# A hybrid mixer and SwiGLU trunk on one core: GpSimd's elementwise work given to VectorE, and one PSUM tile taken from another pool

## The chip, the core and the metric

The kernel runs on one core of a Trainium2 chip. Five engines work from queues of their own: TensorE (PE) multiplies matrices into PSUM, VectorE (DVE) and ScalarE (ACT) read PSUM and do elementwise work, GpSimd (POOL) does elementwise work on SBUF, and SyncE (SP) issues transfers. They meet at semaphores. The metric is the device time of one execution in microseconds, the median of several runs.

## The reference, cut to what matters

Two layers, 512 frames of 1024 channels, float32. Each layer is a token mixer followed by a SwiGLU feed-forward; both are normed before and after and added to the residual. The mixer is one projection whose columns feed three branches:

```python
q, k, v = silu(conv4(dn_qkv)); q, k l2-normed            # 4 heads of 128
beta = sigmoid(dn_b); g = -exp(A_log) * softplus(dn_a + dt_bias)
o_dn = gated_delta_rule(q, k, v, beta, g)                # chunks of 64, a triangular solve in each
o_dn = rms(o_dn) * dn_out_norm * silu(dn_z)
o_pool = mapped(trailing means over 2, 4, 8, 16 frames, minus the frame) * scale
rq, rk = rotary(ret_q), rotary(ret_k)
o_ret = groupnorm(chunkwise_retention(rq, rk, ret_v)) * ret_out_norm * silu(ret_g)
y = sigmoid(g0)*(o_dn @ w_dn) + sigmoid(g1)*(o_pool @ w_pool) + sigmoid(g2)*(o_ret @ w_ret)
x = x + rms_norm(y @ w_out);  x = x + rms_norm(swiglu(rms_norm(x)))
```

Inside a chunk the delta rule solves `(I + M) X = rhs` with a strictly lower triangular `M = (k_beta k^T) * decay`. Retention weights frame j for frame i by gamma^|i-j| within a chunk and by gamma^(i-j) across chunks.

## The kernel before, in words

All activations lie channel by frame: 128 partitions, 512 columns, eight tiles for 1024 channels. A projection (L515 to L522, `project`) makes 128 output channels: eight pieces of 128 input channels, and for each piece three matmuls of 512 columns (`mm3`, L231 to L233), because each float32 operand is held as a rounded high part and a remainder. The weights come as 512 KB tiles over SyncE's queue (L216) and are split in halves of 512 columns: ScalarE rounds (L241, `wh`), VectorE subtracts (L242, `wl`). A PSUM tile `pp` (three buffers) takes a projection, `fx` (two buffers) the small products of retention, pooling and the token gates, `cx` (three buffers) those of the delta rule.

The delta rule (`delta`) is a generator that yields a number of steps; between its parts `fill` advances the lanes `tasks` (projections and what follows them: pooling, rotations, retention, gates, branches), `side` (the attention part of retention) and `late`. So the order in which the program is written comes out of how often each generator yields, and a scheduler then settles the order of every engine's queue, with the weight loads and splits drawn ahead by priorities (`EARLY`, `AHEAD`). Each engine executes its queue in that order, and an instruction that waits holds up what stands behind it.

What the change and the prediction touch:

- `token_gates` (L553): L564 makes the product of the gate columns into `fx`, VectorE scales it (L567, `cv`), TensorE transposes it with selection matmuls (L570) into a second `fx` tile, and ScalarE (L577, `beta`) and VectorE (L579, `sx`) read that tile. The pooling maps L1044 follow in `fx`.
- `sums_of` and the loop behind it (L770, L771, L785 to L787): decays and masks per head, 256 columns each.
- The block inverses of head h are sent through the queue of SyncE into `uc` (L843, four loads per head, 16 in a row). `back` (L934) takes `uc` as `uu` (L944) and runs two level steps per head: transposes L547 and products L960 with a mask `ml` (L938), the product L970, and the subtraction L971 into `uu`.
- `rotated` (L1084) and `retention` (L1098): L1090 to L1094 make `kr` and `qr`. Values are transposed (L547) into a PSUM tile, and their mean is taken off (L1119, L1121, L1123, `vc`). The gate projection gives L1126 and its sigmoid L1128.
- `attention` (L1132): scores L1136 and transposed keys L1138 into two `fx` tiles, read by L1140 (VectorE) and L1141 (ScalarE); the state product L1150 into `fx`; the running states (L1152 on ScalarE, two L1154 on VectorE); L1165 and L1167 for the output.
- `mixed_in` (L1067) adds a branch to `y`.

Of the kernel before, what the change touches and what calls it, by code (L numbers as in the profile page):

```python
# [135 lines left out]
def tile_hybrid(ctx: ExitStack, tc: tile.TileContext, x_in, consts, rot, rmask, vecs, wab, wi, wpl, wbr, wo, wgu, wd, out):  # L136
# [30 lines left out]
    def over(m, n=NT):  # L167

        return m.rearrange("p (o b) -> p o b", o=1).to_broadcast([P, n, m.shape[1]])

    def along(s, width):

        return s.rearrange("p (t o) -> p t o", o=1).to_broadcast([P, s.shape[1], width])
# [29 lines left out]
    def hd(t, n=NT):  # L203
        return t.rearrange("p (t b) -> p t b", t=n)
# [325 lines left out]
    def mixer(l, xd, hs, rb, firsts):  # L530
# [5 lines left out]
        def tl(tag, bufs=1, shape=(P, S), dt=F32):  # L536
            return pool.tile(list(shape), dt, tag=tag, bufs=bufs, name=nm(tag))

        def tiny(tag, n=16):
            return tl(tag, shape=(P, n))  # L540

# [11 lines left out]
        def token_gates():  # L553
            raw = tl("mc", 2, (P, NT * B16))
            nc.scalar.dma_start(out=raw, in_=wab[l])
            G.memset(abw.bitcast(F32), 0.0)
            r8, w8 = raw.rearrange("p (k n) -> p k n", n=8), abw.rearrange("p (k n) -> p k n", n=P)
            V.tensor_copy(out=w8[:, :, 0:8], in_=r8)
            V.tensor_tensor(out=w8[:, :, 8:16], in0=r8, in1=w8[:, :, 0:8].bitcast(F32), op=ALU.subtract)
            yield WAITS["ab"]  # L560
            ps = psum_f()
            for k in range(KT):
                for j in range(2):
                    T.matmul(ps, lhsT=w8[:, k], rhs=hs[k][j], start=k == 0 and j == 0, stop=k == KT - 1 and j == 1)  # L564
            yield
            ab = tl("cv")
            V.tensor_tensor(out=ab[0:16, 0:S], in0=ps[0:16], in1=rb[0:16], op=ALU.mult)  # L567
            pst = psum_o()
            for t in range(NT):
                T.matmul(  # L570
                    pst[:, t * 8 : t * 8 + 8], lhsT=ab[0:16, ts(t)], rhs=kc[0:16, K_SEL : K_SEL + 8], start=True, stop=True
                )
            yield
            abt = pst[:, 0:32].rearrange("p (t n) -> p n t", n=8)

            beta = tiny("beta")
            A.activation(out=beta.rearrange("p (n t) -> p n t", n=4), in_=abt[:, 0:4], func=AF.Sigmoid)  # L577
            sx = tiny("sx")
            V.tensor_tensor(  # L579
                out=sx.rearrange("p (n t) -> p n t", n=4),  # L580
                in0=abt[:, 4:8],
                in1=vec[:, l, V_DTB : V_DTB + 16].rearrange("p (n t) -> p n t", n=4),
                op=ALU.add,
            )

            nab = tiny("nab")
            V.scalar_tensor_tensor(out=nab, in0=sx, scalar=-1.0, in1=sx, op0=ALU.mult, op1=ALU.min)
            e = tiny("e")
            A.activation(out=e, in_=nab, func=AF.Exp)
            ea = tiny("ea")  # L590
            with behind(A.engine):
                A.activation(out=ea, in_=vec[:, l, V_ALOG : V_ALOG + 16], func=AF.Exp)
            den = tiny("den")
            V.tensor_scalar(out=den, in0=e, scalar1=2.0, scalar2=None, op0=ALU.add)
            V.reciprocal(out=den, in_=den)
            yield
            z = tiny("z")
            V.tensor_tensor(out=z, in0=e, in1=den, op=ALU.mult)
            z2 = tiny("z2")
            V.tensor_tensor(out=z2, in0=z, in1=z, op=ALU.mult)  # L600
            po = tl("po", 2, (P, 16))
            V.tensor_scalar(out=po, in0=z2, scalar1=2.0 / 17, scalar2=None, op0=ALU.mult)
            for c in (15, 13, 11, 9, 7, 5, 3):
                po2 = tl("po", 2, (P, 16))
                V.scalar_tensor_tensor(out=po2, in0=po, scalar=2.0 / c, in1=z2, op0=ALU.add, op1=ALU.mult)
                po = po2
            yield
            lp = tiny("lp")
            V.scalar_tensor_tensor(out=lp, in0=po, scalar=2.0, in1=z, op0=ALU.add, op1=ALU.mult)
            sp = tiny("sp")  # L610
            V.scalar_tensor_tensor(out=sp, in0=sx, scalar=0.0, in1=lp, op0=ALU.max, op1=ALU.add)
            g = tiny("g")
            V.scalar_tensor_tensor(out=g, in0=sp, scalar=-1.0, in1=ea, op0=ALU.mult, op1=ALU.mult)
            for _ in range(GATES):
                yield
            pcs = psum_c()
            for n, m in enumerate((c_le, c_gt, c_e0, c_e1)):
                T.matmul(pcs[:, n * 16 : n * 16 + 16], lhsT=m, rhs=g, start=True, stop=True)
            yield
            ex = tiny("ex", 64)  # L620
            A.activation(out=ex, in_=pcs[:, 0:64], func=AF.Exp)
            tok.update(beta=beta, g=g, e_g=ex[:, 0:16], e_tail=ex[:, 16:32], e_last=[ex[:, 32:48], ex[:, 48:64]])
            yield
# [18 lines left out]
        def hc(h):  # L642
            return slice(h * NT, (h + 1) * NT)
# [96 lines left out]
        def delta():  # L740
# [26 lines left out]
            def sums_of(h):  # L767
                rr = tl("c1", 4)
                r3 = rr.rearrange("p (a t b) -> p a t b", a=2, t=NT)
                G.tensor_tensor(out=r3[:, 0], in0=over(gt64), in1=along(g[:, hc(h)], C), op=ALU.mult)  # L770
                G.tensor_tensor(out=r3[:, 1], in0=over(le64), in1=along(g[:, hc(h)], C), op=ALU.mult)  # L771
                return rr

            rr = sums_of(0)
# [1 line left out]
            for h in range(H):  # L776
                ps = psum_c()
                T.matmul(ps[:, 0 : NT * C], lhsT=c_le, rhs=rr[:, 0 : NT * C], start=True, stop=True)
                T.matmul(ps[:, NT * C :], lhsT=c_gt, rhs=rr[:, NT * C :], start=True, stop=True)
                dec = tl("c1", 4)  # L780
                A.activation(out=dec, in_=ps, func=AF.Exp)
                if h + 1 < H:
                    rr = sums_of(h + 1)
                bm = tl("bm", 1, half)
                G.tensor_tensor(out=hd(bm), in0=over(gt64), in1=along(brk2[:, hc(h)], C), op=ALU.mult)  # L785
                G.tensor_tensor(out=ms_[h], in0=dec[:, 0 : NT * C], in1=bm, op=ALU.mult)
                G.tensor_tensor(out=hd(ats[h]), in0=hd(dec[:, NT * C :]), in1=over(le64), op=ALU.mult)  # L787
                yield WAITS["dec"]


# [142 lines left out]
        def back(h, m_, uc, beg, e_tail):  # L933
            def level(v):  # L934
                m = tl("ml", 2)
                for f in range(2):
                    cc = slice(f * C, (f + 1) * C)
                    G.tensor_tensor(out=hd(m)[:, :, cc], in0=hd(m_), in1=over(lvl[v][:, cc]), op=ALU.mult)  # L938
                return hd(m)

            ml = level(LEVELS[0])
# [61 lines left out]
            A.activation(out=sg, in_=t, func=AF.Sigmoid)  # L1003
            res.append(sg)


        tl("gap", shape=(P, 16))

        def operand(name, i, fn):
            a, b = tl("oh", H, dt=F32R), tl("ol", H, dt=F32R)  # L1010
            fn(a, b)
# [43 lines left out]
        def mixed_in(i, name, n, r_):  # L1055
            if n % 2 == 0:
                bw[name] = weights(wbr[l, i, n // 2])
            ps = psum_p()
            yield from products(ps, bw[name], [oh[name, k] for k in range(H)], 4 * (n % 2))
            if name == "p":  # L1060
                y = keep.tile([P, S], F32, tag="y", bufs=KT, name=nm("y"))
                V.tensor_tensor(out=y, in0=ps, in1=r_[0], op=ALU.mult)
                ys[n] = y
            else:
                t = ftc()
                V.tensor_tensor(out=t, in0=ps, in1=r_[0], op=ALU.mult)  # L1066
                G.tensor_tensor(out=ys[n], in0=ys[n], in1=t, op=ALU.add)  # L1067
            yield

        crb, srb = tl("crb"), tl("srb")  # L1070
# [14 lines left out]
        def rotated(b, tag, res):  # L1085
            r_ = []
            yield from project(wi[l, b], hs, r_)
            ps = r_[0]
            t1, t2 = ftc(), ftc()
            V.tensor_tensor(out=t1, in0=ps, in1=crb, op=ALU.mult)  # L1090
            V.tensor_tensor(out=t2[0:C], in0=ps[C:P], in1=srb[C:P], op=ALU.mult)
            V.tensor_tensor(out=t2[C:P], in0=ps[0:C], in1=srb[0:C], op=ALU.mult)
            o = tl(tag)
            G.tensor_tensor(out=o, in0=t1, in1=t2, op=ALU.add)  # L1094
            res.append(o)
            yield


        def retention(h):
# [13 lines left out]
            for _ in range(VT):  # L1113
                next(p)
                yield
            ps = psum_f()
            transposed(v_, ps)
            su = tl("rsu", 2, (P, NT))
            V.tensor_reduce(out=su, in_=hd(ps), axis=AX.X, op=ALU.add)  # L1119
# [12 lines left out]
        def attention(h, mask, kr, qr, vc, t, sg):  # L1132
# [6 lines left out]
            s_sb, kt = ftc(), ftc()[:, 0 : S - P]  # L1139
            V.tensor_tensor(out=hd(s_sb), in0=hd(s_ps), in1=over(mask[:, 0:P]), op=ALU.mult)  # L1140
            A.activation(out=kt, in_=k_ps[:, 0 : S - P], func=AF.Copy, scale=mask[:, 2 * P : 2 * P + 1])  # L1141
            G.tensor_tensor(out=hd(qr), in0=hd(qr), in1=over(mask[:, P : 2 * P]), op=ALU.mult)
            sw = tl("sw")
            V.scalar_tensor_tensor(
                out=sw, in0=t, scalar=vec[:, l, V_RN + h : V_RN + h + 1], in1=sg, op0=ALU.mult, op1=ALU.mult
# [327 lines left out]
```

## Time and the profile before

| | us |
|---|---|
| median of 3 runs | 1832.48 (1831.73 to 1835.91) |
| the profiled execution's own time | 1831.59 |
| its span | 1829.8 |
| TensorE busy in it | 1807.6 (99%) |
| VectorE busy | 1049.8 (57%) |
| ScalarE busy | 719.1 (39%) |
| GpSimd busy | 364.1 (20%) |

The span is the time from the first to the last instruction in the trace; 1.8 us lie around it. Matmuls are pipelined, so their recorded lengths overlap: a 512-column matmul is recorded with about 0.39 us, though the next one starts earlier. An idle stretch before an instruction is given with what ended it, as in "[2.29 <-DVE vc L1123]".

### The profile page before, as it was taken

The numbers are of one execution on the slowest core, as the hardware profiler recorded it, in microseconds if no ns is written. First come the engines' busy times: TensorE is split into PE (matmuls) and PEld (weight loads), VectorE is DVE, ScalarE is ACT, GpSimd is POOL, SyncE is SP. The second block draws the span as 40 slices with busy tenths as digits, with TensorE's granted clock in tenths as the row PEclk, the third lists the DMA queues.
The fourth block names the chain that finished last, engine by engine and source line by source line (L and its number), as shares of the span: only waits on it lengthen the run. The fifth ranks groups of instructions, "written<-read, shape, count | busy, mean of one in ns | idle before, by whom it ended". The sixth has DMA issues, their size and how long they took to land.

```text
span 1829.8 us, 25153 instructions
## 1 busy us (share of the span) xinstructions
PE 1807.6 (99%) x9528; PEld 1538.0 (84%) x9528; DVE 1049.8 (57%) x1924; ACT 719.1 (39%) x1294; POOL 364.1 (20%) x350
## 2 busy tenths in 40 slices
PE   9999999999999999999999999999999999999997
PEld 7788888888898888888987888888888988888887
DVE  7778766674447432444577786676644564324443
ACT  5643333333445332333446433333434443333332
POOL 2040211012133210221210402110121332102212
PEclk9999999999999999999999999999999999999998
DMA  5323212124325333233233222222243252323221
GB/s 187 118 71 95 75 62 79 52 93 138 104 82 182 95 98 98 92 104 93 83 131 97 83 84 74 61 73 62 89 142 121 66 179 93 103 92 101 96 93 47
DMA packets 65849, 177.73 MB, mean 97 GB/s; under 512 B 15424, under 2 KB 19648, under 8 KB 65728
## 3 DMA queue, kind: packets, MB, share of 16 engines
q1 hardware_dynamic: 58800, 173.04, 29.3%
q10 hardware_dynamic: 6928, 3.08, 0.7%
q8 instruction: 75, 1.23, 0.3%
q14 instruction: 46, 0.38, 0.1%
HBM read 167.18 MB, written 8.39 MB: 96 GB/s over the span
## 4 chain that ended last, share of the span: by engine, by line
PE 95%; DVE 3%; issue 1%; ACT 0%; DMA 0%; POOL 0%; ACTq 0%; DVEq 0%
PE pp L231 28%; PE pp L233 28%; PE pp L232 28%; PE cx L232 1%; PE cx L231 1%; PE cx L233 1%; PE cx L876 1%; PE fx L276 1%; PE cx L861 1%; PE cx L960 1%; PE cx L970 1%; PE cx L547 1%; PE cx L801 0%; PE cx L898 0%; DVE xt L354 0%
## 5 line engine op out<-in xcount | busy, mean ns | idle before, releaser
L231 PE MATMUL pp<-hh,wh 128*128 128x512 f32 (+1 forms) x1592 | 628.6, 395 | 0.0
L233 PE MATMUL pp<-hh,wl 128*128 128x512 f32 (+1 forms) x1592 | 616.6, 387 | 0.0
L232 PE MATMUL pp<-hl,wh 128*128 128x512 f32 (+1 forms) x1592 | 615.9, 387 | 0.0
L241 ACT ACTIVATE wh<-raw 128x512 fp32r<-128x512 f32 x570 | 355.9, 630 | 648.6 <-PE pp L232 575.2
L242 DVE TENSOR_TENSOR wl<-raw,wh 128x512 fp32r<-128x512 f32 x570 | 424.8, 750 | 298.7 <-ACT wh L241 287.1
L233 PEld LDWEIGHTS pp<-hh,wl 128*128 128x128 f32 x1592 | 299.0, 188 | 62.4 <-issue 1.0
L231 PEld LDWEIGHTS pp<-hh,wh 128*128 128x128 f32 x1592 | 299.3, 188 | 60.9 <-issue 3.7
L232 PEld LDWEIGHTS pp<-hl,wh 128*128 128x128 f32 x1592 | 299.5, 188 | 57.6 <-issue 1.0
L231 PE MATMUL pp<-ah,wh 128*128 128x512 f32 (+1 forms) x376 | 134.7, 358 | 0.0
L233 PE MATMUL pp<-ah,wl 128*128 128x512 f32 (+1 forms) x376 | 134.4, 357 | 0.0
L232 PE MATMUL pp<-al,wh 128*128 128x512 f32 (+1 forms) x376 | 134.4, 357 | 0.0
L1340 POOL TENSOR_TENSOR gs<-gt,sg 128x512 f32<-128x512 f32 x44 | 57.6, 1310 | 315.2 <-ACT sg L1338 315.2
L1345 POOL TENSOR_TENSOR a<-gs,ut 128x512 f32<-128x512 f32 x44 | 70.8, 1612 | 130.8 <-DVE ut L1343 130.8
L314 POOL TENSOR_TENSOR sqa<-sqa,sq 128x256 f32<-128x256 f32 (+1 forms) x73 | 63.8, 874 | 106.0 <-ACT sq L307 83.6
L231 PEld LDWEIGHTS pp<-ah,wh 128*128 128x128 f32 x376 | 71.0, 189 | 10.4
L232 PEld LDWEIGHTS pp<-al,wh 128*128 128x128 f32 x376 | 71.0, 189 | 10.4
L233 PEld LDWEIGHTS pp<-ah,wl 128*128 128x128 f32 x376 | 71.0, 189 | 10.2
L242 DVE TENSOR_TENSOR al<-a,ah 128x512 fp32r<-128x512 f32 x44 | 33.9, 770 | 74.4 <-ACT ah L241 74.2
L231 PE MATMUL pp<-yh,wh 128*128 128x256 f32 (+1 forms) x224 | 67.1, 300 | 0.0
L233 PE MATMUL pp<-yh,wl 128*128 128x256 f32 (+1 forms) x224 | 66.8, 298 | 0.0
L232 PE MATMUL pp<-yl,wh 128*128 128x256 f32 (+1 forms) x224 | 66.8, 298 | 0.0
L1067 POOL TENSOR_TENSOR y<-y,ft 128x512 f32<-128x512 f32 x16 | 25.1, 1572 | 196.6 <-DVE ft L1066 196.6
(332 smaller groups left out, 2453.8 us busy)
## 6 DMA issues: line engine op xcount, KB each, us to landing
raw<-in_wi_dram SPq DMA_DIRECT2D x117, 512.0 KB
raw<-in_wgu_dram SPq DMA_DIRECT2D x88, 512.0 KB
raw<-in_wd_dram SPq DMA_DIRECT2D x44, 512.0 KB
raw<-in_wbr_dram SPq DMA_DIRECT2D x24, 512.0 KB
raw<-in_wo_dram SPq DMA_DIRECT2D x16, 512.0 KB
xd<-xt SPq DMA_DIRECT2D x24, 256.0 KB
xt<-xd SPq DMA_DIRECT2D x24, 256.0 KB
xt<-in_x_dram SPq DMA_DIRECT2D x16, 256.0 KB
```

Source lines behind the costliest of these rows:

```text
L231: T.matmul(ps, lhsT=w[0], rhs=m[0], start=start, stop=False)
L232: T.matmul(ps, lhsT=w[0], rhs=m[1], start=False, stop=False)
L233: T.matmul(ps, lhsT=w[1], rhs=m[0], start=False, stop=stop)
L241: A.activation(out=hi, in_=src, func=AF.Copy)
L242: V.tensor_tensor(out=lo, in0=src, in1=hi.bitcast(F32), op=ALU.subtract)
L276: T.matmul(ps[:, t : t + 1], lhsT=sq[:, ts(t)], rhs=one, start=i == 0, stop=i == len(sqs) - 1)
L314: G.tensor_tensor(out=t, in0=acc[0], in1=acc[1], op=ALU.add)
L547: T.transpose(ps[:, ts(t)], src[:, ts(t)], ident)
L861: T.matmul(tmp[:, ts(h)], lhsT=pair(h, t, 2 * f), rhs=state[:, ts(h)], start=True, stop=True,)
L1067: G.tensor_tensor(out=ys[n], in0=ys[n], in1=t, op=ALU.add)
L1340: G.tensor_tensor(out=gs, in0=gt, in1=sg, op=ALU.mult)
L1345: G.tensor_tensor(out=a, in0=gs, in1=ut, op=ALU.mult)
```

## The change

It has four parts. In the mixer the elementwise operations of L770, L771, L785, L786, L787, L938, L1067, L1094 and L1142 are issued on VectorE rather than GpSimd. In `retention` the transposed values are written to a tile of the pool `pp` rather than of `fx`. `token_gates` yields three times rather than once behind its product. And two groups of tiles (`oh`, `ol`) are allocated at the front of their pool while a 16-column tile (`gap`) is dropped, which concerns addresses alone. GpSimd keeps L1082 and its work outside the mixer's core.

```diff
         def tl(tag, bufs=1, shape=(P, S), dt=F32):
             return pool.tile(list(shape), dt, tag=tag, bufs=bufs, name=nm(tag))
+        for tag in ("oh", "ol"):
+            tl(tag, H, dt=F32R)
...
                     T.matmul(ps, lhsT=w8[:, k], rhs=hs[k][j], start=k == 0 and j == 0, stop=k == KT - 1 and j == 1)
-            yield
+            for _ in range(3):
+                yield
             ab = tl("cv")
...
-                G.tensor_tensor(out=r3[:, 0], in0=over(gt64), in1=along(g[:, hc(h)], C), op=ALU.mult)
-                G.tensor_tensor(out=r3[:, 1], in0=over(le64), in1=along(g[:, hc(h)], C), op=ALU.mult)
+                V.tensor_tensor(out=r3[:, 0], in0=over(gt64), in1=along(g[:, hc(h)], C), op=ALU.mult)
+                V.tensor_tensor(out=r3[:, 1], in0=over(le64), in1=along(g[:, hc(h)], C), op=ALU.mult)
...
-                G.tensor_tensor(out=hd(bm), in0=over(gt64), in1=along(brk2[:, hc(h)], C), op=ALU.mult)
-                G.tensor_tensor(out=ms_[h], in0=dec[:, 0 : NT * C], in1=bm, op=ALU.mult)
-                G.tensor_tensor(out=hd(ats[h]), in0=hd(dec[:, NT * C :]), in1=over(le64), op=ALU.mult)
+                V.tensor_tensor(out=hd(bm), in0=over(gt64), in1=along(brk2[:, hc(h)], C), op=ALU.mult)
+                V.tensor_tensor(out=ms_[h], in0=dec[:, 0 : NT * C], in1=bm, op=ALU.mult)
+                V.tensor_tensor(out=hd(ats[h]), in0=hd(dec[:, NT * C :]), in1=over(le64), op=ALU.mult)
...
-                    G.tensor_tensor(out=hd(m)[:, :, cc], in0=hd(m_), in1=over(lvl[v][:, cc]), op=ALU.mult)
+                    V.tensor_tensor(out=hd(m)[:, :, cc], in0=hd(m_), in1=over(lvl[v][:, cc]), op=ALU.mult)
...
-        tl("gap", shape=(P, 16))
...
-                G.tensor_tensor(out=ys[n], in0=ys[n], in1=t, op=ALU.add)
+                V.tensor_tensor(out=ys[n], in0=ys[n], in1=t, op=ALU.add)
...
-            G.tensor_tensor(out=o, in0=t1, in1=t2, op=ALU.add)
+            V.tensor_tensor(out=o, in0=t1, in1=t2, op=ALU.add)
...
-            ps = psum_f()
+            ps = psum_p()
             transposed(v_, ps)
...
-            G.tensor_tensor(out=hd(qr), in0=hd(qr), in1=over(mask[:, P : 2 * P]), op=ALU.mult)
+            V.tensor_tensor(out=hd(qr), in0=hd(qr), in1=over(mask[:, P : 2 * P]), op=ALU.mult)
```

The new lines shift the numbers: in the rows of the change below, a line is 4 higher than in the kernel before from L540 to L565, 5 higher up to L1004, and 2 higher behind that. The text goes by the numbers of the kernel before. In a row of an order, `a<-b` are the program's names for what is written and read, and the bracket lists the queues that it waits for.

**VectorE, retention of head 0.** First the kernel before, from the last block reduction (L835) over the mean of the values to the running states (L1154):

```order
L835 TENSOR_REDUCE c_408_1658<-c_461_1865 128x15 [waits DVE_49]
L242 TENSOR_TENSOR wl_2242<-raw_2238,wh_2241 128x512 [waits DMAHW5_49,PE_49,Activation_49]
L1119 TENSOR_REDUCE rsu_1909<-fx_1904 128x4 [waits PE_49]
L1121 TENSOR_SCALAR rmu_1911<-rsu_1909 128x4 [waits DVE_49]
L1123 TENSOR_TENSOR vc_1913<-fx_1904,rmu_1911 128x512 [waits DVE_49]
L1126 TENSOR_TENSOR ft_1921<-pp_1854,rb_137 128x512 [waits PE_49]
L242 TENSOR_TENSOR wl_2271<-raw_2238,wh_2270 128x512 [waits Activation_49]
L1140 TENSOR_TENSOR ft_1934<-fx_1925,mask_1741 128x512 [waits PE_49,Pool_49]
L1144 SCALAR_TENSOR_TENSOR sw_1939<-ft_1921,vec,ft_1923 128x512 [waits Activation_49]
L1154 SCALAR_TENSOR_TENSOR ft_1958<-ft_1958,fx_1954 128x128 [waits Activation_49]
L1154 SCALAR_TENSOR_TENSOR ft_1958<-ft_1958,fx_1954 128x128 [waits DVE_49]
```

Then the same place in the change (L1121 to L1125 are the mean and `vc`, L1146 is `sw`, L1156 the running states, L949 takes `uc`):

```order
L1121 TENSOR_REDUCE rsu_1910<-pp_1905 128x4 [waits PE_49]
L1123 TENSOR_SCALAR rmu_1912<-rsu_1910 128x4 [waits DVE_49]
L1125 TENSOR_TENSOR vc_1914<-pp_1905,rmu_1912 128x512 [waits DVE_49]
L1128 TENSOR_TENSOR ft_1922<-pp_1855,rb_137 128x512 [waits PE_49]
L242 TENSOR_TENSOR wl_2272<-raw_2239,wh_2271 128x512 [waits Activation_49]
L1142 TENSOR_TENSOR ft_1935<-fx_1926,mask_1742 128x512 [waits PE_49]
L1144 TENSOR_TENSOR qr_1799<-qr_1799,mask_1742 128x512
L1146 SCALAR_TENSOR_TENSOR sw_1940<-ft_1922,vec,ft_1924 128x512 [waits Activation_49]
L949 TENSOR_TENSOR uu_2039<-uc_1875,kc 128x512 [waits DMAHW2_49,DMAHW3_49,DMAHW1_49,DMAHW0_49]
L1156 SCALAR_TENSOR_TENSOR ft_1959<-ft_1959,fx_1955 128x128 [waits Activation_49]
L949 TENSOR_TENSOR uu_2046<-uc_1880,kc 128x512 [waits DMAHW6_49,DMAHW7_49,DMAHW5_49,DMAHW4_49]
L1156 SCALAR_TENSOR_TENSOR ft_1959<-ft_1959,fx_1955 128x128 [waits DVE_49]
```

The mean now reads `pp` instead of `fx`. The product L1142 of `qr` has come in, and two L944 that wait for four loads each stand in front of the two L1154; before, they stood some two dozen rows later. Further ahead in VectorE's queue, between the block reductions, the two sums of L1094 for `kr` and `qr` have come in too, and the split L242 that followed the last L835 now precedes it.

**TensorE, the level steps of heads 0 and 1.** Before, from the first level's products L970 to the second level's transposes L547 and products L960:

```order
L970 MATMUL cx_2136<-c_520_2080,c_519_2078 128x128 [waits Activation_49]
L970 MATMUL cx_2136<-c_520_2080,c_519_2078 128x128 x3
L970 MATMUL cx_2142<-c_525_2097,c_524_2095 128x128 [waits Activation_49]
L970 MATMUL cx_2142<-c_525_2097,c_524_2095 128x128 x3
L547 MATMUL cx_2175<-ident,uu_2038 128x128 [waits DVE_49]
L547 MATMUL cx_2175<-ident,uu_2038 128x128 x3
L960 MATMUL cx_2176<-uu_2038,ml_2082 128x128 [waits PE_49,Pool_49]
L960 MATMUL cx_2176<-uu_2038,ml_2082 128x128 x3
L547 MATMUL cx_2189<-ident,uu_2045 128x128 [waits DVE_49]
```

In the change (L975 is L970, L551 is L547, L965 is L960; the rows left out are twelve matmuls of a projection):

```order
L975 MATMUL cx_2137<-c_521_2081,c_520_2079 128x128 [waits Activation_49]
L975 MATMUL cx_2137<-c_521_2081,c_520_2079 128x128 x3
L975 MATMUL cx_2143<-c_526_2098,c_525_2096 128x128 [waits Activation_49]
L975 MATMUL cx_2143<-c_526_2098,c_525_2096 128x128 x3
...
L551 MATMUL pp_2170<-ident,cv_2034 128x128 [waits DVE_49]
L551 MATMUL pp_2170<-ident,cv_2034 128x128 x3
L551 MATMUL cx_2176<-ident,uu_2039 128x128 [waits DVE_49]
L551 MATMUL cx_2176<-ident,uu_2039 128x128 x3
L965 MATMUL cx_2177<-uu_2039,ml_2083 128x128 [waits PE_49]
L965 MATMUL cx_2177<-uu_2039,ml_2083 128x128 x3
```

Twelve matmuls and four transposes of `cv` now stand between L970 and the transposes of the updated `uu`, where before nothing did. On VectorE four of the masks L938 and the first L1094 stand around the L668 ahead of L971, and two splits L242 that stood before L971 stand behind it.

**TensorE, the token gates of layer 1.** Before, from the selection matmuls L570 to the first pooling maps (left out: nine matmuls of the projection):

```order
L233 MATMUL pp_8919<-hh_8203,wl_8921 128x512
L570 MATMUL fx_8955<-kc,cv_8953 128x8 [waits DVE_49,Activation_49]
L570 MATMUL fx_8955<-kc,cv_8953 128x8 x3
L231 MATMUL pp_8919<-hh_8205,wh_8960 128x512
L232 MATMUL pp_8919<-hl_8206,wh_8960 128x512
...
L233 MATMUL pp_8919<-hh_8211,wl_8961 128x512
L1044 MATMUL fx_9024<-kr_8831,sw_8820 128x512 [waits DMAHW4_49,PE_49]
L1044 MATMUL fx_9036<-qr_8840,sw_8820 128x512 [waits DVE_49]
L231 MATMUL pp_9063<-hh_8197,wh_9064 128x512
```

In the change (L575 is L570, L1046 is L1044):

```order
L232 MATMUL pp_8921<-hl_8213,wh_8955 128x512
L233 MATMUL pp_8921<-hh_8212,wl_8956 128x512
L575 MATMUL fx_8988<-kc,cv_8986 128x8 [waits DVE_49,Activation_49]
L575 MATMUL fx_8988<-kc,cv_8986 128x8 x3
L1046 MATMUL fx_8993<-kr_8833,sw_8822 128x512 [waits DMAHW4_49,PE_49]
L231 MATMUL pp_9058<-hh_8198,wh_9059 128x512 [waits DVE_49]
L232 MATMUL pp_9058<-hl_8199,wh_9059 128x512
L233 MATMUL pp_9058<-hh_8198,wl_9060 128x512
L1046 MATMUL fx_9012<-qr_8842,sw_8822 128x512 [waits DVE_49]
```

All eighteen matmuls behind L564 now precede L570, where before six did and twelve followed. On VectorE `sx` (L579) used to stand before two L242 and an L658; now it stands behind them. On ScalarE `beta` (L577) stood before the two sigmoids L1003 of layer 1 and now stands behind them.

## Rows read from the trace of the kernel before

**Rows 1.** The page: busy time by engine, chain of waits by engine
```profile
PE 1807.6 (99%) x9528; PEld 1538.0 (84%) x9528; DVE 1049.8 (57%) x1924; ACT 719.1 (39%) x1294; POOL 364.1 (20%) x350
...
PE 95%; DVE 3%; issue 1%; ACT 0%; DMA 0%; POOL 0%; ACTq 0%; DVEq 0%
```

**Rows 2.** Waits of PE: line waited for: us in total, times, longest
```profile
PE fx L1138 <- DVE vc L1123: 4.6, 2, 2.3
PE cx L547 <- DVE uu L971: 2.4, 2, 1.2
...
PE fx L570 <- DVE cv L567: 1.1, 1, 1.1
```

**Rows 3.** Page, VectorE's weight split L242; busy, mean ns, idle before
```profile
L242 DVE TENSOR_TENSOR wl<-raw,wh 128x512 fp32r<-128x512 f32 x570 | 424.8, 750 | 298.7 <-ACT wh L241 287.1
```

**Rows 4.** Timeline 175 to 183 us, VectorE and GpSimd: start, us, line, tile
```profile
175.75 1.79 DVE L242 TENSOR_TENSOR wl<-raw,wh 128x512 fp32r<-128x512 f32 x1
178.27 0.68 DVE L242 TENSOR_TENSOR wl<-raw,wh 128x512 fp32r<-128x512 f32 x1
...
175.69 1.30 POOL L1094 TENSOR_TENSOR kr<-ft,ft 128x512 f32<-128x512 f32 x1 [29.75 <-DVE ft L1092]
```

**Rows 5.** Groups by line on GpSimd: busy us, mean ns; idle before
```profile
L1094 POOL TENSOR_TENSOR kr<-ft,ft 128x512 f32<-128x512 f32 x8 | 12.1, 1515 | 107.8 <-DVE ft L1092 107.8
...
L938 POOL TENSOR_TENSOR ml<-m__260_1054,kc 128x256 f32<-128x256 f32 x4 | 3.3, 842 | 15.8 <-PE cx L960 15.8
```

**Rows 6.** Stretches, busy of PE, PEld, DVE, ACT, POOL (instructions); clock, DMA, GB/s
```profile
159.70:195.00 35.30, 33.01 (x170) 27.06 (x168) 34.09 (x83) 9.64 (x16) 3.93 (x3) 1.00 0.27 78
199.60:216.80 17.20, 16.00 (x97) 13.77 (x96) 16.53 (x31) 6.63 (x12) 4.84 (x5) 1.00 0.30 93
288.90:307.20 18.30, 18.30 (x86) 14.92 (x85) 17.60 (x32) 5.64 (x9) 3.01 (x2) 1.00 0.22 66
```

**Rows 7.** Timeline, retention of head 0 in layer 0, TensorE: start, us, line
```profile
189.36 1.05 PE L1136 MATMUL fx<-qr,kr 128*128 128x128 f32 x8
192.71 0.52 PE L1138 MATMUL fx<-ident,kr 128*128 128x128 f32 x3 [2.29 <-DVE vc L1123]
...
194.46 0.89 PE L1150 MATMUL fx<-vc,ft 128*128 128x128 f32 x6
...
197.92 0.39 PE L1167 MATMUL fx<-ft,qr 128*128 128x128 f32 x2
```

**Rows 8.** Timeline, the same stretch, VectorE and ScalarE
```profile
189.03 0.39 DVE L835 TENSOR_REDUCE c<-c 128x15 f32<-128x225 f32 x1
...
190.65 1.18 DVE L1121 TENSOR_SCALAR rmu<-rsu 128x4 f32<-128x4 f32 x1
191.87 0.69 DVE L1123 TENSOR_TENSOR vc<-fx,rmu 128x512 f32<-128x512 f32 x1
...
193.79 0.56 ACT L1141 ACTIVATE ft<-fx,mask 128x384 f32<-128x384 f32 x1
```

**Rows 9.** Timeline, SyncE queue: uc loads; ScalarE queue and VectorE: mc load
```profile
189.45 10.58 SPq L843 DMA_DIRECT2D uc<-c  x16
...
938.51 0.44 ACTq L555 DMA_DIRECT2D mc<-in_wab_dram  x1
...
943.16 0.20 DVE L558 CAST abw<-mc 128x64 fp32r<-128x64 f32 x1 [2.34 <-DMA mc<-in_wab_dram]
```

**Rows 10.** Timeline, level steps of heads 0 and 1: TensorE, VectorE
```profile
213.05 2.01 PE L970 MATMUL cx<-c,c 128*128 128x128 f32 x16
...
215.52 1.27 DVE L971 TENSOR_TENSOR uu<-uu,cx 128x512 f32<-128x512 f32 x2
```

**Rows 11.** Timeline, token gates of layer 1: TensorE, VectorE
```profile
955.75 1.02 PE L570 MATMUL fx<-kc,cv 16*128 16x8 f32 x8 [1.14 <-DVE cv L567]
...
959.58 1.02 PE L1044 MATMUL fx<-kr,sw 128*128 128x512 f32 x2
...
958.69 0.15 DVE L579 TENSOR_TENSOR sx<-fx,vec 128x16 f32<-128x16 f32 x1
```

## The prediction

> **What bounds the kernel now.** I read the page first: TensorE is busy for 99% of the span and makes 95% of the chain that ends last [rows 1]. So only what TensorE waits for can be won, or more lost; the change leaves its matmuls as they are. The second view is the list of TensorE's waits. Three of its entries lie where the change works: L1138 on `vc`, twice 2.3 us, once per layer; L547 on `uu` (L971), twice 1.2 us; L570 on `cv`, once, 1.1 us [rows 2]. Together 8.1 us, or 0.44%: the most that the change can take away. The third reading is why VectorE is late there. Its weight split L242 has a mean of 750 ns [rows 3], but at 175.75 one took 1.79 us and at 178.27 another 0.68; the long one started 60 ns behind GpSimd's L1094, which took 1.30 [rows 4]. This stretch has the pattern twice. So an SBUF operation of GpSimd stops VectorE's for nearly its whole length. The fourth reading says where VectorE has no room: in three stretches of layer 0 it is busy for 34.1 of 35.3, 16.5 of 17.2 and 17.6 of 18.3 us [rows 6].
>
> **The prices.** A 512-column sum costs GpSimd 1.52 us [rows 5]; VectorE runs two such operations in 1.27 [rows 10], 0.6 each. 40 of these move (16 of L1067, 16 of L1094, 8 of L1142), so 24 us. 72 of 256 columns move (32 of L938, eight each of L770, L771, L785 to L787); L938 costs GpSimd 0.84 [rows 5]. VectorE needs 0.15 for 16 columns [rows 11] and 0.68 for 512 [rows 4], so on a line about 0.41 recorded, 0.33 from start to start: 24 us. VectorE thus takes on some 48 us over both layers and gets back about 1.1 us for each split that no longer stands beside a GpSimd operation. Neither is on the path by itself; what counts is what stands ahead of the three waits.
>
> **Place A, retention of head 0, -0.95 us per layer.** Today L1138 would be ready at 190.42 and starts at 192.71 [rows 7], since its `fx` tile is still read by L1123, the subtraction that makes `vc` [rows 8]. With the values in `pp` this wait goes. What is late next? L1150 needs `vc` and the keys that ScalarE copies in L1141. Without the wait, TensorE wants it at 190.42 plus today's 1.75 from L1138 to L1150, so 192.17. VectorE: the last L835 ends at 189.42 today [rows 8]. Two splits lose 1.11 us each, two L1094 come in at 0.6, one L242 moves ahead at 0.6: 189.0. From there to `vc` it is 2.45 today; L242 (0.6) is gone from between, and L1121, a 4-column operation of 1.18 us beside GpSimd's L1142 [rows 8], falls to about 0.2. So `vc` starts at about 189.9, and L1141 ends 2.48 later as today (191.87 to 194.35 [rows 8]), at 192.4. Some links I may have too short, so I take a wait of 0.5 (0.2 to 0.9) and L1150 at 192.65.
>
> Then the added wait: two L944 now stand ahead of the two L1154, and the second needs the eighth load of `uc`. What is queued behind it on VectorE is L1154, and the third L1167 of TensorE waits for that. Sixteen loads take 10.58 us to issue, 0.66 each, and the first starts when the last L835 is done [rows 9]; so the eighth starts at about 193.7. No row shows its landing. Below it is bounded by its own issue, 0.66; above by the `mc` load, issued at 938.51 and awaited until 943.16, 4.6 us [rows 9]. That one comes from DRAM between weight tiles, `uc` is 8 KB within the chip, so I take 2.3, nearer to the lower row. Landed at 196.0, plus L944 0.6 and L1154 0.3, gives 196.95 for the third L1167, which TensorE would want at 192.65 + 3.46 = 196.1 and reaches at 197.92 today [rows 7]. Gain 0.95, two layers: -1.9 us. With 0.66 nothing waits and it is -3.6; with 4.6 L1167 comes at 199.2 and it is +2.6. The sum is zero at a landing time of 3.3 us.
>
> The trace has one case of a VectorE instruction at the head of its queue that waits for a load: L558, with the engine idle for 2.34 us [rows 9]. The Trainium skill, "PSUM — Partial Sum Buffer", section "Engine vs sequencer instructions", says that VectorE's queue is strictly first in, first out. The row agrees; if L1154 could pass L944, place A would give -3.6, and by the rule it gives what is written above.
>
> **Place B, the level steps of heads 0 and 1, -1.2 us per layer.** L970 starts at 213.05 and takes 2.01; L971 runs from 215.52, two in 1.27 [rows 10], and L547 waits 1.20 for the first. In the change twelve matmuls (0.23 each: six take 1.4 between L1138 and L1150) and four transposes of `cv` stand between, 3.4 us. L547 is then wanted 5.4 us behind L970's start; the first L971 ended 3.1 behind it. On VectorE four L938 (1.3 us) come in ahead, two L242 of 0.6 move behind, and GpSimd no longer stops them. That leaves about 2 us of room, the cover of the L938 here. I book -2.4 for both layers; the other end is 0, if VectorE comes 2.3 us later than I think.
>
> **Place C, token gates, -0.6 us.** In layer 1 L570 starts at 955.75 after 1.14 of waiting [rows 11]. With twelve more matmuls ahead it is wanted at 954.6 + 2.75 = 957.35, and `cv` is long done. But the pooling map of `qr` needs the tile that L579 reads, and L579 moves behind an L242 and an L658: from 958.69 [rows 11] to 959.9, done at 960.05. TensorE wants it after L570 (1.07), one map (0.9) and three matmuls (0.7), at 960.0. ScalarE's `beta`, which L579 waits for, stands behind two sigmoids now. I take a wait of 0.3 (0 to 1.1), so -0.8. Layer 0 has no wait at L570 today; the same new order costs 0 to 0.5 there, taken as 0.2.
>
> **The rest.** L1067, the decays, and the later heads stand where TensorE has projections that don't depend on them, so I cost them at nothing; that cover fails if their splits L242 come late (last rival). For small waits that I can't place I add 0.4, between 0 and 1.2, the shortest per-layer wait that goes. Addresses alone: 0.
>
> **The sum.** -1.9 - 2.4 - 0.6 + 0.4 = -4.5 us. Against the profiled execution's 1831.59 that is 1827.1. The median shown is 1832.48, 0.9 above, so I predict 1828.0. A measurement of this kernel tells about 0.2% from no change, 3.7 us.
>
> **The rivals.**
> - *All three waits go, nothing comes in their place* (`uc` lands within 1.5 us, `vc` is early): -8.1, so 1824.4. For it: a transfer of 8 KB is small. Against: the chain from `vc` to L1141 alone needs 2.48 us.
> - *The wait at A only changes its name* (`uc` lands late, up to 4.6 us): A is 0 to +2.6, the total -2.6 to 0, so 1830 to 1832.5, taken as 1831. For it: weight tiles share the transfer engines. Nothing that can be measured.
> - *VectorE becomes the bound.* If the long splits are not caused by GpSimd, nothing is paid back. In the three stretches of rows 6 GpSimd is busy for 3.9, 4.8 and 3.0 us; on VectorE that is 0.6/1.52 of it, 4.6 us per layer in stretches with 0.7 to 1.2 us of idle time each. Both layers: +9.3, of which TensorE's loss is all but B and C's gains, so about +6 and 1839. It decides once more than 1.2 us net come in per stretch. Against it: the start of the long split just behind L1094 and its end 0.55 behind that one's end [rows 4].
>
> For the last one the rows show 1.11 us lost beside a GpSimd operation of 1.30. The Trainium skill, "SBUF — State Buffer", section "SBUF: two separate sides", says that the two engines take a shared port pair as an exclusive lock for a whole instruction. The trace agrees; by that rule the 1.11 us come back in full, and without it the sum is the last rival's.
>
> **How the numbers follow.** The forecast has 0.5, of which 0.4 lies below 1828.8 and 0.1 above; all waits gone 0.1; the wait renamed 0.3; VectorE the bound 0.1. So faster by over 0.2%: 0.5; within 0.2%: 0.4; slower: 0.1. The likeliest's own range, from the bounds at A and C, is 1826 to 1830.5. The range 1823.8 to 1834 takes in the first rival and the second and leaves out the third.
>
> **What would show it.** Right: no wait at L1138 for `vc`, a wait under 1 us at L1150 and one at the third L1167 for L1154 with VectorE idle ahead of the second L944 on `uc`; no wait at the second level's L547; none at L570, a short one at the map of `qr`; L242's mean near 0.69; GpSimd's busy time down by some 120 us (40 x 1.52 and 72 x 0.84) and VectorE's about the same. Wrong: an L242 mean still at 750, waits of TensorE on L242 or on `uu` in these stretches, or as much waiting of TensorE in sum as before.

## The result, and the profile after

The changed kernel takes 1824.21 us (median of 4 runs, 1823.74 to 1824.56) against 1832.9 for the kernel before in the same comparison (1831.73 to 1835.91): a ratio of 0.9948, interval 0.9936 to 0.996, so 0.4 to 0.64% faster. I had said 1828.0, 0.24% faster: the right sign, about half the size.

The two profiled executions differ by less than the medians: 1831.59 against 1824.56 us, 7.0. The medians are 8.7 apart. Both have to be explained.

The page of the changed kernel, busy time by engine, answers to [rows 1]; then all waits of TensorE (line waited for: us in total, times, longest), which answer to [rows 2]; then the split L242 of [rows 3].

```profile
PE 1807.2 (99%) x9528; PEld 1538.1 (84%) x9528; DVE 1065.2 (58%) x2036; ACT 716.9 (39%) x1294; POOL 249.7 (14%) x238
```
```profile
PE fx L1169 <- DVE ft L1156: 1.5, 2, 0.8
PE cx L232 <- DVE hl L238: 1.7, 3, 0.6
PE fx L300 <- DVE rsz L289: 1.3, 1, 1.3
PE fx L388 <- DVE eps L398: 1.2, 1, 1.2
PE fx L276 <- ACT sq L307: 0.8, 1, 0.8
PE cx L231 <- ACT wh L241: 0.3, 1, 0.3
```
```profile
L242 DVE TENSOR_TENSOR wl<-raw,wh 128x512 fp32r<-128x512 f32 x570 | 405.8, 717 | 289.2 <-ACT wh L241 278.1
```

The first stretch of [rows 6], found again at 158.9 in this trace (same columns):

```profile
158.90:194.00 35.10, 35.10 (x181) 28.93 (x180) 33.15 (x88) 10.18 (x17) 0.00 (x0) 1.00 0.28 79
```

TensorE's own work is as before, and in that stretch it has no idle time left. GpSimd is busy for 114 us less. VectorE is busy for only 15 more, though it has taken on 112 operations: the splits alone gave back 19 us (424.8 to 405.8, a mean of 750 to 717 ns). The three waits of [rows 2] are gone, 8.1 us, and one has come, 1.5; the other five entries stand in the kernel before too, at the norms and the start. In sum the waits fell by 6.7 of the 7.0 us.

Place A, retention of head 0, TensorE first, then VectorE and SyncE's queue (start, us, line; L1138, L1152 and L1169 are L1136, L1150 and L1167 of before, L840 is L835, L1125 is `vc`, L1142 is L1140, L949 is L944, L1156 is L1154). They answer to [rows 7 to 9]:

```profile
189.27 1.05 PE L1138 MATMUL fx<-qr,kr 128*128 128x128 f32 x8
...
192.03 0.94 PE L1152 MATMUL fx<-vc,ft 128*128 128x128 f32 x6
...
196.50 0.49 PE L1169 MATMUL fx<-ft,qr 128*128 128x128 f32 x2 [0.80 <-DVE ft L1156]
```
```profile
188.33 0.38 DVE L840 TENSOR_REDUCE c<-c 128x15 f32<-128x225 f32 x1
...
189.35 0.17 DVE L1123 TENSOR_SCALAR rmu<-rsu 128x4 f32<-128x4 f32 x1
189.55 0.69 DVE L1125 TENSOR_TENSOR vc<-pp,rmu 128x512 f32<-128x512 f32 x1
...
191.35 0.68 DVE L1142 TENSOR_TENSOR ft<-fx,mask 128x512 f32<-128x512 f32 x1
...
193.82 0.28 DVE L1156 SCALAR_TENSOR_TENSOR ft<-ft,fx 128x128 f32<-128x128 f32 x1
195.55 0.69 DVE L949 TENSOR_TENSOR uu<-uc,kc 128x512 f32<-128x512 f32 x1 [1.45 <-DMA uc<-c]
196.16 0.28 DVE L1156 SCALAR_TENSOR_TENSOR ft<-ft,fx 128x128 f32<-128x128 f32 x1
```
```profile
188.74 9.27 SPq L848 DMA_DIRECT2D uc<-c  x14
```

The reader is to see L1123 at 0.17 us, where its like took 1.18 beside GpSimd; `vc` at 189.55, 2.3 us earlier; L1152 without a wait; and then VectorE standing still for 1.45 us for `uc`, ahead of the L1156 for which the third L1169 waits 0.80. That L1156 needs only what the first one had finished at 194.10, and still it ran at 196.16, behind the L949 that waited. The eighth load was issued seven times 0.66 behind 188.74, at 193.4, and L949 had it at 195.55: it took 2.2 us.

Place B, the level steps, TensorE then VectorE (L975 is L970, L551 is L547, L976 is L971), to be read with [rows 10]:

```profile
208.38 1.95 PE L975 MATMUL cx<-c,c 128*128 128x128 f32 x16
...
213.33 0.60 PE L551 MATMUL cx<-ident,uu 128*128 128x128 f32 x4
```
```profile
211.30 0.69 DVE L976 TENSOR_TENSOR uu<-uu,cx 128x512 f32<-128x512 f32 x1
```

The transposes come 4.95 us behind the start of L975; in the kernel before TensorE asked for them 2.0 behind it. The subtraction that they need was finished at 211.99, 1.3 before. It did not come sooner: it starts 2.92 us behind L975, and in the kernel before it was 2.47 behind L970 [rows 10]. The wait went because TensorE asks later. Place C, layer 1, with [rows 11] (L575 is L570, L1046 the maps, L584 is L579):

```profile
954.68 1.05 PE L575 MATMUL fx<-kc,cv 16*128 16x8 f32 x8
955.67 1.13 PE L1046 MATMUL fx<-kr,sw 128*128 128x512 f32 x2
...
957.34 1.02 PE L1046 MATMUL fx<-qr,sw 128*128 128x512 f32 x2
```
```profile
956.52 0.15 DVE L584 TENSOR_TENSOR sx<-fx,vec 128x16 f32<-128x16 f32 x1
```

No wait at L575, and L584 is done 0.7 us before the map of `qr` starts at 957.34.

### The profile page after: what moved, and what is told of

The parts are those of the page before. It is cut to its first block, busy times and chain, and to the rows that moved or that the text cites. A ratio compares the mean times of both kernels' runs of the same rounds, so it can differ in the third digit from the quotient of the medians.

```text
span 1822.8 us, 25057 instructions
## 1 busy us (share of the span) xinstructions
PE 1807.2 (99%) x9528; PEld 1538.1 (84%) x9528; DVE 1065.2 (58%) x2036; ACT 716.9 (39%) x1294; POOL 249.7 (14%) x238
## 4 chain that ended last, share of the span: by engine, by line
PE 94%; DVE 4%; issue 1%; SPq 0%; ACT 0%; DMA 0%; POOL 0%; ACTq 0%; DVEq 0%
PE pp L231 27%; PE pp L233 27%; PE pp L232 27%; PE cx L232 1%; PE cx L233 1%; PE cx L231 1%; PE cx L881 1%; PE cx L965 1%; PE cx L975 1%; PE fx L276 1%; PE cx L866 1%; DVE wl L242 1%; PE cx L551 1%; PE cx L806 0%; PE cx L903 0%
## 5 line engine op out<-in xcount | busy, mean ns | idle before, releaser
L242 DVE TENSOR_TENSOR wl<-raw,wh 128x512 fp32r<-128x512 f32 x570 | 405.8, 717 | 289.2 <-ACT wh L241 278.1
L1276 POOL TENSOR_TENSOR yf<-gt,y 128x512 f32<-128x512 f32 x16 | 26.7, 1672 | 390.1 <-DVE gt L1274 390.1
L242 DVE TENSOR_TENSOR al<-a,ah 128x512 fp32r<-128x512 f32 x44 | 33.9, 770 | 74.3 <-ACT ah L241 74.0
```

The source lines that it names most:

```text
L242: V.tensor_tensor(out=lo, in0=src, in1=hi.bitcast(F32), op=ALU.subtract)
L1276: G.tensor_tensor(out=y, in0=t, in1=ys[n], op=ALU.add)
```

## The experiments

Each was timed in five rounds beside the kernel before; ratios are to it. They are numbered in the order in which they ran.

**One part alone, four times.** The tile of `pp` alone (experiment 1):

```diff
-            ps = psum_f()
+            ps = psum_p()
             transposed(v_, ps)
```

> The kernel before with one edit: the transposed values of retention go to a tile of pp. Theory 1 (VectorE's lateness is what TensorE waits for): the wait at L1138 goes, but vc is as late as before, so L1150 waits instead; vc starts at 191.87 and L1141 ended 2.48 later, while L1150 is wanted at 192.17. The 2 x 2.3 us at L1138 come back as about 2 x 2.1 at L1150; the time falls by 0 to 0.6 us. Rival (the fx buffer is the cause): both waits go, 4 to 4.6 us less, about 1828.

Measured: 1832.65, ratio 0.9998 (0.9989 to 1.0007). Its first wait:

```profile
PE fx L1150 <- DVE ft L1140: 4.6, 2, 2.3
```

The 4.6 us at L1138 are at L1150 now, to the tenth, as theory 1 had it. The tile was not what made TensorE wait; VectorE was, late with `vc` and with L1140, which stands behind `vc` in its queue and now releases L1150.

The nine lines on VectorE alone (2; the `G.` to `V.` lines of the change):

> The kernel before with one edit: the nine GpSimd lines on VectorE. Theory 1: vc is done about 1.6 us earlier, so the wait at L1138 falls from 2.3 to under 0.4 although its tile is still of fx; the wait at L547 for L971 goes; the wait at L570 stays at 1.1; a wait of about 0.8 at the third L1167 comes in. Time 5 to 6 us under the kernel before. Rival (the fx buffer is the cause): the wait at L1138 stays above 1.5 and the gain is 2 to 3 us.

Measured: 1825.15, ratio 0.9956 (0.9944 to 0.9969), span 1823.1. Two waits stand where the change works (L1167 is the wait for `uc`):

```profile
PE fx L1167 <- DVE ft L1154: 1.5, 2, 0.8
...
PE fx L570 <- DVE cv L567: 0.8, 1, 0.8
```

No wait at L1138 with the tile still in `fx`, none at L547. As theory 1 had it; by the spans the gain is 6.7 us where 5 to 6 were forecast, by the medians 8.0.

The three yields alone (3; `for _ in range(3): yield` behind L564):

> The kernel before with one edit: three yields in the token gates. Theory 1: the wait at L570 in layer 1 goes and no wait takes its place; 1.1 to 1.4 us less, the waits at L1138 and L547 as before. Rival (what I forecast): a wait of 0.3 at the qr map and 0.2 in layer 0 come in, 0.6 less.

Measured: 1834.06, ratio 0.9999 (0.9991 to 1.0008). The wait at L570 is gone, but two of 0.3 came, one of them the wait at the map that I had forecast. (The other, at an L547 for `cv`, also stands in the profile of experiment 4, without the yields.) On the median it can't be told from no change. The layout alone (4; `oh` and `ol` first, `gap` dropped):

> The kernel before with one edit: oh and ol allocated first, the 16-column tile dropped; every engine's order is as before. Theory 1: no change, 0 within 1 us. Rival (the 1.7 us by which the medians fell more than the profiled executions come from addresses): 1.5 to 2 us less.

Measured: 1832.69, ratio 0.9998 (0.999 to 1.0007): nothing.

**The change with one part taken back.** The tile back in `fx` (5; `psum_p` to `psum_f`):

> The changed kernel with the transposed values back in fx. Theory 1: vc is early enough by the VectorE moves alone (it ended at 190.24 in the changed kernel, and L1138 started at 190.16), so L1138 waits at most 0.3 us per layer; the time is that of the changed kernel plus 0 to 0.6 us. Rival (tile and moves both are needed): L1138 waits over 1 us again, 2 us or more slower than the changed kernel.

Measured: 1824.1, ratio 0.995 (0.9938 to 0.9962), the same list of waits as the changed kernel. Beside the VectorE moves the tile does nothing.

Decays and branch sums back on GpSimd (7; `V.` to `G.` in L770, L771, L785 to L787, L1067):

> The changed kernel with the decays (L770, L771, L785 to L787) and the branch sums (L1067) back on GpSimd; only L938, L1094 and L1142 stay on VectorE. Theory 1: these three lines stand ahead of the three waits, the others ahead of none; the same time as the changed kernel within 0.7 us. Rival (all contention with GpSimd costs, wherever it stands): 1.5 to 4 us slower than the changed kernel.

Measured: 1823.86, ratio 0.9949 (0.9937 to 0.9961). Theory 1 held. So L938, L1094 and L1142 are the whole of the move's worth; what GpSimd takes from VectorE elsewhere costs nothing that can be measured. L1094 and L1142 were not taken apart. Only the masks back on GpSimd (10; `V.` to `G.` in L938):

> The changed kernel with the masks L938 alone back on GpSimd; by that TensorE has the second level's transposes right behind L970 again. Theory 1: the wait of L547 for L971 is back with 0.5 to 1.3 us per layer, place A stays as in the changed kernel; 1 to 2.7 us slower than the changed kernel. Rival (the wait came from L1094 beside the splits): no wait at L547, the time of the changed kernel.

Measured: 1825.79, ratio 0.9958 (0.9946 to 0.9971). Place B's wait is back (L551 is L547), though L1094 was on VectorE:

```profile
PE cx L551 <- DVE uu L976: 2.7, 2, 1.3
```

With the masks on GpSimd TensorE's queue has the transposes right behind the product again, and GpSimd's masks run beside VectorE's splits again. This run alone doesn't separate the two; experiment 9, which has GpSimd's masks and the other order, has no wait. The old order with the masks on VectorE was not run.

**The wait that came in.** L944 of heads 0 and 1 on GpSimd (6):

```diff
             with behind(V.engine) if h < 2 else ExitStack():
-                V.tensor_tensor(
+                (G if h < 2 else V).tensor_tensor(
```

> The changed kernel with the two L944 of heads 0 and 1 on GpSimd, so that their wait for the uc loads holds no VectorE queue. Theory 1: the wait at the third L1167 (0.8 per layer) goes, 1.2 to 1.6 us less than the changed kernel, about 1822.7. Rival: GpSimd's two operations of some 1.3 us stop VectorE's splits or L1154 for as long, and nothing is won or up to 1 us lost.

Measured: 1822.36, ratio 0.9942 (0.9929 to 0.9954), span 1820.6; the wait is gone and none came, as theory 1 had it. This is the lowest median of all, though its interval overlaps that of the changed kernel. The loads in another order (11):

```diff
-            for h in range(H):
+            for h in (0, 2, 1, 3):
                 uc = tl("uc", H, (P, NT * B16))
```

> The changed kernel with the uc loads in the order of heads 0, 2, 1, 3, so that head 1's land 2.6 us later; the second L944 then stands behind both L1154 in VectorE's queue. Theory 1 (the wait at L1167 came from L944 standing ahead of L1154, not from anything that needs the load early): although the load is later, the wait of 0.8 per layer goes and 1.2 to 1.6 us are won against the changed kernel. Rival: the later load makes TensorE wait at the level steps of head 1, 1 to 4 us slower.

Measured: 1824.79, ratio 0.9953 (0.9941 to 0.9966). The wait at L1167 went, as theory 1 had it, and one at the level step came, as the rival had it. Its wait, then VectorE, then ScalarE (L967 copies the first level's transposes):

```profile
PE cx L965 <- ACT c L967: 2.9, 2, 1.4
```
```profile
197.60 0.69 DVE L949 TENSOR_TENSOR uu<-uc,kc 128x512 f32<-128x512 f32 x1 [2.65 <-DMA uc<-c]
198.21 0.68 DVE L1176 TENSOR_REDUCE rsu<-ft 128x4 f32<-128x512 f32 x1
...
202.01 0.68 DVE L663 TENSOR_TENSOR ft<-pp,rb 128x512 f32<-128x512 f32 x1
```
```profile
196.02 0.63 ACT L1174 ACTIVATE ft<-ft 128x512 f32<-128x512 f32 x1
...
202.79 0.72 ACT L670 ACTIVATE ct<-ft,vec 128x512 f32<-128x512 f32 x1 [1.50 <-DVE ft L663]
203.42 0.58 ACT L967 ACTIVATE c<-cx 128x512 f32<-128x512 f32 x1
```

ScalarE is done with L1174, the square of the retention output, at 196.65, but its sum on VectorE, L1176, stands behind the second L949, which held the engine for 2.65 us. From L1176 to L663 VectorE works without a wait, ScalarE's L670 waits for L663, and L967 stands behind L670. In the changed kernel L1176 started at 198.31 and L967 at 203.52, so this chain is no later here than there; but TensorE comes to the level step 1.6 us earlier (the transposes at 200.69 against 202.29), 0.8 of it by the wait that is gone, and the load keeps the chain from coming earlier with it. The load, the twelfth in the queue, was issued at 195.45 and had at 197.60, again 2.2 us. One late load reached TensorE through three queues, and ate what the removed wait had given.

**The clock.** To bring back a wait with GpSimd idle, the subtraction L1123 was done five times over for head 0 (8):

```diff
-            V.tensor_tensor(out=hd(vc), in0=hd(ps), in1=along(mu, P), op=ALU.subtract)
+            for _ in range(5 if h == 0 else 1):
+                V.tensor_tensor(out=hd(vc), in0=hd(ps), in1=along(mu, P), op=ALU.subtract)
```

> The changed kernel with the subtraction that makes vc done five times over for head 0, so that TensorE waits again at L1150 for some 3 us per layer; GpSimd is as idle as in the changed kernel. Theory 2 (a wait of over 2 us at this place lets TensorE's clock fall to its lower level in part of the executions): 5 to 7 us more by the waits, and beyond that a spread of 3 us or more between executions, mean clocks from 0.998 down to 0.995, and the lower level in the rows around 190 to 200 or 1095 to 1105. Rival (the spread of the kernel before comes from GpSimd's operations): 5 to 7 us more, a spread below 1.5 us, the clock as in the changed kernel.

Measured: 1822.84, ratio 0.9942 (0.993 to 0.9954): both theories missed. With the longer chain the scheduler made another order, twenty matmuls of a projection ahead of the state product instead of six, so that TensorE had work until 194.98 (L1153 is that product; VectorE's row is the last of the five):

```profile
194.98 0.91 PE L1153 MATMUL fx<-vc,ft 128*128 128x128 f32 x6
```
```profile
194.16 0.68 DVE L1126 TENSOR_TENSOR vc<-pp,rmu 128x512 f32<-128x512 f32 x1
```

Both L944 came later too and found `uc` landed, and the list of waits has no L1167. With extra work the median is below the changed kernel's. That says nothing of the clock, but much of the order, which the next one (9) takes without the moves to VectorE: the kernel before, GpSimd with all its work, the tile, the yields of the token gates, and

```diff
-            yield
+            for _ in range(3 if h == 0 else 1):
+                yield
             kv = psum_f()
```

> The kernel before, GpSimd keeping all nine lines, with the tile of pp, the three yields of the token gates, and three yields rather than one ahead of the state product L1150 of head 0, which puts twelve more matmuls ahead of it. Theory 2 (what counts are TensorE's waits of over a microsecond and the clock that falls behind them in some executions, not GpSimd's sharing as such): L1150 waits under 0.6, L570 not, 5 to 8 us less than the kernel before in the median, and a spread of under 3 us. Rival (GpSimd's operations cost wherever they stand): less than 3 us won, the spread of the kernel before (6 us) stays.

Measured: 1824.23, ratio 0.9951 (0.9937 to 0.9964), runs from 1823.53 to 1825.54. Theory 2 held for the waits and the spread; 8.7 us were won where 5 to 8 were forecast. VectorE and TensorE at place A (L1122, L1124, L1139 and L1152 are L1121, L1123, L1138 and L1150), and the split's group:

```profile
190.77 1.21 DVE L1122 TENSOR_SCALAR rmu<-rsu 128x4 f32<-128x4 f32 x1
192.01 0.69 DVE L1124 TENSOR_TENSOR vc<-pp,rmu 128x512 f32<-128x512 f32 x1
```
```profile
190.37 0.49 PE L1139 MATMUL fx<-ident,kr 128*128 128x128 f32 x3
...
194.79 0.83 PE L1152 MATMUL fx<-vc,ft 128*128 128x128 f32 x6
```
```profile
L242 DVE TENSOR_TENSOR wl<-raw,wh 128x512 fp32r<-128x512 f32 x570 | 422.0, 745 | 297.4 <-ACT wh L241 286.5 <-PE pp L232 8.1 <-PE fx L276 1.6
```

GpSimd is as busy as before (363.9 us), the small operation beside it still takes 1.21, the splits 745 ns, `vc` is as late as ever, and TensorE does not wait. With the tile of `pp`, twelve matmuls moved ahead of the state product do there what nine lines on VectorE did. The tile belongs to it: TensorE asks for L1139 at 190.37, and VectorE reads the values for the last time in L1124, until 192.70; with the values in `fx`, as in the kernel before, that request would have had to wait. The order without the tile was not run. By the same two yields a like group of matmuls and transposes comes to stand between L970 and the second level's L547 at place B, whose wait is gone too.

The clock itself shows in the profile of the tile alone, whose execution took 1835.39. Stretches of 2 us at place A: busy time of PE, PEld, DVE, ACT, POOL (instructions), then the granted clock, the share of the DMA engines, GB/s. Below it TensorE's rows there:

```profile
190.00:192.00 2.00, 1.77 (x10) 1.18 (x8) 1.93 (x3) 0.00 (x0) 1.28 (x1) 1.00 0.42 139
192.00:194.00 2.00, 0.00 (x0) 0.00 (x0) 2.00 (x5) 1.07 (x2) 0.00 (x0) 1.00 0.11 13
194.00:196.00 2.00, 1.92 (x8) 1.82 (x9) 0.69 (x2) 0.28 (x2) 0.00 (x0) 0.54 0.29 67
196.00:198.00 2.00, 2.00 (x8) 1.60 (x7) 0.57 (x2) 0.21 (x2) 0.00 (x0) 0.61 0.16 24
198.00:200.00 2.00, 2.00 (x18) 1.91 (x17) 0.69 (x1) 0.84 (x2) 0.10 (x1) 1.00 0.11 13
```
```profile
194.08 1.63 PE L1150 MATMUL fx<-vc,ft 128*128 128x128 f32 x6 [2.32 <-DVE ft L1140]
...
195.93 0.63 PE L232 MATMUL pp<-hl,wh 128*128 128x512 f32 x1
196.36 0.63 PE L233 MATMUL pp<-hh,wl 128*128 128x512 f32 x1
```

TensorE stands still for 2.32 us, and behind that the granted clock is 0.54 and 0.61 of full speed: at 1.2 GHz, half, for 1.84 and 1.56 of the 2 us each, 3.4 us. The matmuls come 0.43 apart rather than 0.23. In the profiled execution of the kernel before the same wait stands and the clock stays up:

```profile
194.00:196.00 2.00, 2.00 (x13) 1.64 (x12) 1.31 (x3) 0.64 (x2) 0.00 (x0) 1.00 0.15 23
```

So it falls behind such a wait in some executions and not in others, and not even behind each one of an execution. The profiled execution of experiment 3 (1834.06) has the lower clock behind the wait in layer 0 (same columns), and 1.00 from 1100 to 1110, where the same 2.3 us stand in layer 1:

```profile
190.00:200.00 10.00, 7.71 (x43) 6.72 (x42) 6.56 (x11) 2.32 (x5) 1.26 (x1) 0.83 0.26 73
```

In that of experiment 1 it is low behind both, and a third time somewhat behind the 1.1 us at L570. That this shorter wait is the cause is not shown, and what decides was not settled.

```profile
956.00:960.00 4.00, 3.07 (x15) 2.66 (x16) 4.00 (x11) 2.31 (x4) 0.10 (x1) 0.84 0.02 4
960.00:964.00 4.00, 4.00 (x12) 2.56 (x10) 1.99 (x5) 1.63 (x3) 0.10 (x1) 0.73 0.43 131
```

The times go with the clock: of the kernel before, 27 executions beside the first four experiments lie between 1830.68 (mean clock 0.997) and 1837.14 (0.994). With 2.3 us waits in the program, experiments 1, 3 and 4 spread likewise, 1829.82 to 1836.38. Of these four kernels' 80 executions (all 47 of the kernel before beside the experiments), 52 have a mean clock of 0.996 or less; of the 45 of the changed kernel and experiments 2 and 5 to 11, where no wait passes 1.5 us, two have 0.996 and none less. One of the two is the slowest of experiment 6 (1824.95), so the long waits are not all that moves the clock. No slower execution of the kernel before was profiled: that its clock falls at these places is argued from experiments 1 and 3.

## Why the prediction was half right

*What bounds the kernel* held: the three waits went, 8.1 us, and of the change nothing but the forecast wait at L1167 reached TensorE. That L1067 and the decays cost nothing held (experiment 7), and so did the addresses (4). That GpSimd's operations lengthen VectorE's held: L1121 fell to 0.17 us and the splits' mean to 717 ns.

*Place A* was put at -1.9 and is -3.1 by the waits. The renamed wait was sized well (0.85 forecast, 0.80 measured; landing 2.3 against 2.2), and for the reason given, an L1154 held behind an L944. The mis-sized term is the wait of 0.5 at L1150 that I added because some links might be too short: my own chain gave 0.2, and the list of waits has none. It was caution, not a row. The chain's last link was another, too: I let L1150 wait for ScalarE's keys (L1141), but in experiment 1 VectorE's L1140 releases it, which reads the scores out of the `fx` buffer that L1150 writes next; in the changed kernel L1152 starts as that reading ends (192.03).

*Place B* was put at -2.4 and is -2.4, with 1.3 us of room where I had about 2. Of what I gave as its causes, the masks' engine is the one that decides (experiment 10), and by the order that comes of it: the subtraction is no earlier behind L975 than it was, and in experiment 9 the masks are GpSimd's, the order is the changed kernel's kind, and there is no wait.

*Place C* was put at -0.6 and is -1.1. The wait at the map exists, at the 0.3 forecast, where GpSimd keeps its lines (experiment 3), but not beside the moved ones.

*The rest* was put at +0.4 and is -0.4. Nothing came in; of the 0.4 the list of waits shows 0.1, the remainder I can't place.

Together -7.0 where I had -4.5, against the profiled execution. *The step that failed* is, first, what I added for waits that no row showed: 0.5 per layer at L1150, 0.5 at place C, 0.4 for the rest, 1.9 of the 2.5 us. The changed kernel's list has none of them. The second is "the median shown is 1832.48, 0.9 above, so I predict 1828.0". I moved the median by the profile's sum as if the distance between them were the same on both sides. It belongs to the clock: where the waits let it fall, an execution pays up to 6 us more. The kernel before lies 1.3 above its profiled execution in the median, the changed one 0.4 below. Those 1.7 us are the rest of the 8.7 between the medians. That the lower clock comes behind the long wait is shown in the rows of experiments 1 and 3; that it makes up these 1.7 us is argued from the spread, and which of the waits causes how much of it was not separated.

Of the rivals, "all three waits go, nothing comes" (1824.4) named the time almost to the microsecond, but by luck: one wait did come, the waits fell by 6.7 and not 8.1, and the clock made up for it. "VectorE becomes the bound" fell; the first stretch of [rows 6] has VectorE busy for less than before.

Nor are all parts of the change needed. Beside the move to VectorE the tile does nothing (experiment 5), and without the move, the tile and the order give 1824.23 with GpSimd at full work (experiment 9).

## What to carry to other kernels

A wait of TensorE has two sides, when the operand is ready and when TensorE asks. Look first at what independent work could stand ahead of the request: here matmuls put ahead of the requests, with one tile taken from another pool, were worth as much as nine instructions moved to another engine. When an edit moves an operand's wait, list what else stands in that engine's queue behind each wait on a load. And where a profiled execution has waits of some microseconds, look at the spread of the runs and their clocks before taking its sum for the median's.

## What the runs showed that I had not expected

Behind a wait of 2.3 us on TensorE its granted clock was low for 3.4 us in some executions and not in others (0.54 against 1.00 in the same stretch), and in one execution in layer 0 and not in layer 1. At half speed that is another 1.7 us on top of the 2.3. And doing the same subtraction five times over took 1.4 us off the median, since the scheduler's new order had no wait left for `uc`.
